# Splitting each weight slab with one cast and one subtraction of 128x2048 instead of two of each of 128x1024

## The chip, the cores and the metric

The kernel runs on one core of one Trainium2 chip. The metric is the device time of one execution in microseconds. Shown is the median of three timed runs; a profile of one further execution tells where its time goes.

## The reference

A causal decoder trunk of two layers over 256 tokens of width 2048, in float32. Cut to its core:

```python
for layer in range(DEPTH):                       # 2 layers
    h = _rmsnorm(x, mix_norm_g[layer])
    if layer % 2 == 0:                           # latent attention and causal pooling
        c_q, c_kv, k_rope, u_pool = jnp.split(h @ even_w_in[e], split_at, axis=-1)
        a = _mla(c_q, c_kv, k_rope, cos, sin, ...)      # widens the latents by w_uq, w_ukv, then attends
        b = _pool_mixer(u_pool, even_pool_w[e], even_pool_scale[e])
        x = x + jnp.concatenate([a, b], axis=-1) @ even_w_out[e]
    else:                                        # gated short convolution
        x = x + _short_conv(h, odd_w_in[o], odd_conv_w[o], odd_w_out[o])
    x = x + _mlp(_rmsnorm(x, mlp_norm_g[layer]), w_mlp_up[layer], w_mlp_down[layer])   # 2048 -> 8192 -> 2048
```

## The kernel before

**Tiling.** TensorE multiplies in fp32r, so each float32 matrix is written as a sum of two parts: `hi`, the value cast to fp32r, and `lo`, the rest. A product then takes hi times hi, hi times lo and lo times hi. Weights come from HBM as slabs of 1 MB: one DMA on SyncE's queue fills a `raw` tile of 128 partitions by 2048 floats, which is four row tiles of 128x512 (or eight of 128x256). `slab` (L123) issues the DMA and calls `halved` (L132), which splits the slab: for each part of `sub` row tiles, ScalarE casts it into a `hi` tile (L141) and VectorE subtracts into a `lo` tile (L142). Before, a part is half a slab, 128x1024, so a slab takes two casts and two subtractions. Only the eight slabs of the latent projection at the start are split otherwise (two parts of 128x1088, the first one in three pieces).

**Buffers.** `new_stage` (L77) opens the pools: `raws` has three buffers of 8 KB a partition, and `halves` has, for each of `hi` and `lo`, six buffers of 4 KB. A `hi` tile may be written again when TensorE has read its last use; a `raw` tile may be filled again when the last subtraction from it is done.

**Stages.** First the latent projection (L153), up to about 65 us. Then the pooling projection (L464): four groups of channels g = 3, 2, 1, 0, each of two slabs of eight row tiles; they are called G1 to G8 here. After each group VectorE takes the result from PSUM into `pu` (L479), GpSimd sums it over shifted copies into `pm` (L486 to L493), and ScalarE and VectorE split that (L201, L202). Then `widen` (L515) multiplies the latents by four slabs of w_ukv and three of w_uq, called W1 to W4 and Q1 to Q3: ScalarE takes each result out of PSUM (L522) and sums squares of it (L508), VectorE and GpSimd make the scale `rk` of it (L536, L277, L278), and VectorE applies it (L543, L546). Then come the pooling mixer with one slab, the attention mixed with the output projection, the MLP of layer 0 (about 300 to 940 us), the convolution, and the MLP of layer 1 (about 1355 to 1990 us).

**The MLP.** Sixteen chunks of 512 hidden columns go two and two. `up_chunk` (L719) multiplies four slabs of w_up; after each chunk its result is taken out of PSUM (`sum_halves`, L192), put through ReLU and the square (L732, L734) and split into `hT` (L201, L202), and sums of it into `fT`. `down_seven` (L751) makes a 2x2 block product of w_down in seven products instead of eight (`product`, L768, lines L772 to L774), from slabs and from blocks `t` and `v` to which GpSimd's queue adds further blocks of w_down while loading. The generators are called in an order written out by hand, which puts a slab of `up_chunk` (16 pairs of L161 and L162) behind each product (12 matmuls).

**Order.** Each engine runs its instructions in one order, fixed when the program is built, from the order in the code, the readiness of operands and buffers, and an estimate of durations. An instruction that waits holds up all that stand behind it on its engine.

Of the kernel before, what the change touches and what calls it, by code (L numbers as in the profile page):

```python
# [16 lines left out]
P = 128  # L17
# [15 lines left out]
GROUPS = 4  # L33
# [34 lines left out]
def trunk(ctx: ExitStack, tc, x_in, pos_in, mix_g, mlp_g, w_up, w_down, w_in, qa_g, kva_g, w_uq, w_ukv,  # L68
# [5 lines left out]
    big = ctx.enter_context(tc.tile_pool(name="big", bufs=1))  # L74
    stage = []

    def new_stage(raw_bufs=0, **more):  # L77

        for s_ in reversed(stage[1 - bool(raw_bufs):]):
            s_.close()  # L80
        del stage[1 - bool(raw_bufs):]
        for wanted in (dict(raws=raw_bufs, halves=6) if raw_bufs else {}, more):
            if wanted:
                stage.append(ExitStack())
                for name, bufs in wanted.items():
                    pools[name] = stage[-1].enter_context(tc.tile_pool(name=uid(name), bufs=bufs, reuse_waits="tile"))
# [8 lines left out]
    def uid(s):  # L95
        count[0] += 1
        return f"{s}{count[0]}"

    def bank2():
        return psum.tile([P, 2, 512], F32, tag="ps", name=uid("ps"))  # L100
# [6 lines left out]
    def flush():  # L107

        todo = waiting[:]
        waiting.clear()  # L110
        for f in todo:
            f()
# [7 lines left out]

    last_prep = []

    def slab(src, kt, cols, sub=2, dmas=1, pieces=None):  # L123

        raw = pools["raws"].tile([P, kt, cols], F32, tag="raw", name=uid("raw"))
        rows_ = src.rearrange("(k p) n -> p k n", p=P)
        for i in range(dmas):
            n = kt // dmas
            nc.sync.dma_start(raw[:, i * n:(i + 1) * n, :], rows_[:, i * n:(i + 1) * n, :])
        return halved(raw, sub, pieces)  # L130

    def halved(raw, sub=2, pieces=None):  # L132

        kt, cols = raw.shape[1], raw.shape[2]
        out_ = []
        for i in range(0, kt, sub):
            hi = pools["halves"].tile([P, sub, cols], F32R, tag="hi", name=uid("hi"))
            lo = pools["halves"].tile([P, sub, cols], F32R, tag="lo", name=uid("lo"))
            for c0, n in pieces if pieces and i == 0 else ((0, cols),):
                r, h, l = (w[:, :, c0:c0 + n] for w in (raw[:, i:i + sub, :], hi, lo))  # L140
                a = nc.scalar.copy(h, r)  # L141
                v = nc.vector.tensor_tensor(out=l, in0=r, in1=h.bitcast(F32), op=ALU.subtract)  # L142
            last_prep[:] = [a, v]
            out_ += [(hi[:, j, :], lo[:, j, :]) for j in range(sub)]
        return out_
# [12 lines left out]
    def columns_out(o, act, kt, w, c0, first, last):  # L158

        hi, lo = w  # L160
        nc.tensor.matmul(o, lhsT=hi[:, c0:c0 + P], rhs=act[:, kt, :], start=first, stop=False)  # L161
        nc.tensor.matmul(o[:, S:2 * S], lhsT=lo[:, c0:c0 + P], rhs=act[:, kt, 0:S], start=False, stop=last)  # L162

    def columns_summed(o, act, kt, w, c0, first, last):

        hi, lo = w
        nc.tensor.matmul(o, lhsT=hi[:, c0:c0 + P], rhs=act[:, kt, 0:S], start=first, stop=False)  # L167
        nc.tensor.matmul(o, lhsT=hi[:, c0:c0 + P], rhs=act[:, kt, S:2 * S], start=False, stop=False)  # L168
        nc.tensor.matmul(o, lhsT=lo[:, c0:c0 + P], rhs=act[:, kt, 0:S], start=False, stop=last)  # L169

    def columns_chunk(w, xT, c0, n):

        pss = []
        for _ in columns_steps(pss, w, xT, c0, n):
            pass
        return pss

    def columns_steps(pss, w, xT, c0, n):

        pss.extend(bank2() for _ in range(n // 2))  # L180
        rows_ = 16 // n
        for s in range(KD // rows_):
            ws = slab(w[s * rows_ * P:(s + 1) * rows_ * P, c0:c0 + n * P], rows_, n * P, sub=rows_ // 2)
            for j in range(rows_):
                kt = s * rows_ + j
                for i in range(n):
                    columns_out(pss[i // 2][:, i % 2, :], xT, kt, ws[j], i * P, kt == 0, kt == KD - 1)
            if s == 0:
                flush()
            yield  # L190
# [20 lines left out]
    attn = ExitStack()  # L211
    ap_ = attn.enter_context(tc.tile_pool(name="attn", bufs=1, side="right"))
    ctx.callback(lambda: [s_.close() for s_ in reversed(stage)])
    new_stage(3)


    x = big.tile([P, T, D], F32, tag="x", name="x")
# [105 lines left out]
    def twice(a):  # L323

        return a.unsqueeze(1).to_broadcast([P, 2, S])
# [9 lines left out]
    def latent_slab(s, insts=()):  # L335
        with behind(*insts):
            slabs.append(slab(w_in[0, s * 2 * P:(s + 1) * 2 * P, 0:LAT], 2, LAT, sub=1,
                              dmas=2 if s == 0 else 1, pieces=cuts if s == 0 else None))
# [3 lines left out]
    for s in range(8):  # L342
        if s:
            latent_slab(s)
        ws = slabs[s]
# [4 lines left out]
        for j in range(2):  # L350
            kt = 2 * s + j
# [40 lines left out]
    R0 = []  # L392
    waiting.append(latents)
    new_stage(3)

    PAD = 16
# [60 lines left out]
    def split_pooled(g, m):  # L457
        c, k = g // 2, 2 * (g % 2)
        if c not in pooledT:
            pooledT[c] = act_tile()  # L460
        split(pooledT[c][:, k:k + 2, 0:S], pooledT[c][:, k:k + 2, S:2 * S], m)

    done = None
    for g in reversed(range(GROUPS)):  # L464
        ps = bank2()
        for s in range(2):
            c0 = LAT + g * 2 * P
            ws = slab(w_in[0, s * 8 * P:(s + 1) * 8 * P, c0:c0 + 2 * P], 8, 2 * P, sub=4)
            for j in range(8):
                kt = 8 * s + j  # L470
                for n in range(2):
                    columns_summed(ps[:, n, 0:S], xT, kt, ws[j], n * P, kt == 0, kt == KD - 1)
            if s == 0:
                flush()
        if done:
            split_pooled(*done)
        u = ap_.tile([P, 2, PAD + S], F32, tag="s", name=uid("pu"), bufs=4)
        nc.gpsimd.memset(u[:, :, 0:PAD], 0.0)
        nc.vector.tensor_tensor(out=u[:, :, PAD:], in0=ps[:, :, 0:S], in1=twice(R0[0]), op=ALU.mult)  # L479
        cur = u  # L480
        for st in range(g + 1):
            sh = 1 << st
            nxt = ap_.tile([P, 2, PAD + S], F32, tag="s", name=uid("pn"), bufs=4)
            if st < g:
                nc.gpsimd.memset(nxt[:, :, 0:PAD], 0.0)
            nc.gpsimd.tensor_tensor(out=nxt[:, :, PAD:], in0=cur[:, :, PAD:], in1=cur[:, :, PAD - sh:PAD + S - sh],  # L486
                                    op=ALU.add)
            cur = nxt
        m = small.tile([P, 2, S], F32, tag="u", name=uid("pm"))
        nc.gpsimd.tensor_scalar(out=m, in0=cur[:, :, PAD:], scalar1=1.0 / (2 << g), scalar2=None, op0=ALU.mult)  # L490
        nc.gpsimd.tensor_tensor(out=m[:, :, 0:PAD], in0=cur[:, :, PAD:2 * PAD],
                                in1=invc[:, g, :].unsqueeze(1).to_broadcast([P, 2, PAD]), op=ALU.mult)
        nc.gpsimd.tensor_tensor(out=m, in0=m, in1=u[:, :, PAD:], op=ALU.subtract)  # L493
        done = g, m
# [34 lines left out]
    for b in range(4):  # L529
        widen(w_ukv, latT[0], 1, b, QW)  # L530
        tot = small.tile([P, T, 2], F32, tag="tot2", name=uid("tot"))
        for t in range(T):
            for h in (2 * b, 2 * b + 1):
                c0 = QW + h * (NOPE + VD)
# [39 lines left out]


    mixed = {}
    ws = slab(pool_w[0].rearrange("g c d -> (g c) d"), 2 * GROUPS, 2 * P, sub=4)
    for c in range(2):
        mt = act_tile()
        mixed[2 + c] = mt  # L580
        for i in range(2):
            g = 2 * c + i
# [129 lines left out]
    def mlp(layer, ss, xT, after=None):  # L712
        up, down = w_up[layer], w_down[layer]
        hid, sums, totals = {}, {}, {}
        r2 = []
        new_stage(blocks=1, forms=2)
        pairs = DFF // NB // 2

# [32 lines left out]
        def down_seven(pair):  # L751
# [16 lines left out]
            def product(o, b, left):  # L768

                for q, (hi, lo) in enumerate(halved(b)):  # L770
                    a_hi, a_lo = left(2 * pair + q // 2, q % 2)
                    nc.tensor.matmul(o, lhsT=a_hi, rhs=hi, start=q == 0, stop=False)  # L772
                    nc.tensor.matmul(o, lhsT=a_hi, rhs=lo, start=False, stop=False)  # L773
                    nc.tensor.matmul(o, lhsT=a_lo, rhs=hi, start=False, stop=q == 3)  # L774
# [207 lines left out]
```

## Time and profile before

| | |
|---|---|
| timed runs | 2027.75, 2026.78, 2024.16 us; median 2026.78 us |
| profiled execution | 2025.33 us, of which the span from the first to the last instruction is 2023.5 us |
| TensorE (PE) | 2005.9 us busy, 10534 matmuls |
| VectorE (DVE) | 1389.5 us busy, 1739 instructions |
| ScalarE (ACT) | 1120.1 us busy, 1480 instructions |
| GpSimd (POOL) | 124.4 us busy |
| DMA | 457.62 MB, 226 GB/s over the span |
| granted TensorE clock | 0.998 on the mean |

The matmuls overlap, so their busy time is a union and not a sum. The chain of work that ended last consists to 98% of matmuls. What counts is therefore the time at which TensorE stands still, and which engine it then waits for; the idle time of the other engines costs nothing by itself.

### The profile page before, as it was taken

Reading aid. Unit: us, or ns where it says so; the run is one execution under the profiler, and the core shown is the slowest. Engines: PE = TensorE matmul, PEld = TensorE weight load, DVE = VectorE, ACT = ScalarE, POOL = GpSimd, SP = SyncE. Lnnn points to the kernel's source line nnn. Section 1 sums busy time; section 2 is a strip of 40 time slices with the busy share of each in tenths; the row PEclk is TensorE's granted clock in tenths of the full one; section 3 lists DMA queues with packets and bytes.
Section 4 is the critical chain, followed back from the end, with each engine's and each line's share of the span. In section 5 each row is a group of like instructions: output and inputs, shape, how many; then the busy total and the mean of one; then the engine's idle time right before and its main releaser. Section 6 shows DMA issues by size and latency. Waiting matters only on the chain.

```text
span 2023.5 us, 26714 instructions
## 1 busy us (share of the span) xinstructions
PE 2005.9 (99%) x10534; PEld 1722.5 (85%) x10534; DVE 1389.5 (69%) x1739; ACT 1120.1 (55%) x1480; POOL 124.4 (6%) x132
## 2 busy tenths in 40 slices
PE   8999999999999999999999999999999999999999
PEld 7987888888888888888888888888888888888887
DVE  5767567677766777776666656567777777777774
ACT  5457456565555655555444444456555566555552
POOL 2240000000000000000000000000000000000000
PEclk9999999999999999999999999999999999999999
DMA  7555577998989889865555557758898988989773
GB/s 245 161 173 177 182 219 215 270 247 242 281 252 264 245 258 257 263 208 187 179 190 188 190 191 226 231 177 222 267 255 265 270 239 265 257 253 270 217 224 125
DMA packets 232782, 457.62 MB, mean 226 GB/s; under 512 B 7344, under 2 KB 17456, under 8 KB 232656
## 3 DMA queue, kind: packets, MB, share of 16 engines
q1 hardware_dynamic: 202704, 396.91, 58.5%
q0 software_dynamic: 29920, 59.00, 17.1%
q8 instruction: 82, 1.34, 0.3%
q14 instruction: 44, 0.36, 0.0%
q10 hardware_dynamic: 32, 0.01, 0.0%
HBM read 453.79 MB, written 2.10 MB: 225 GB/s over the span
## 4 chain that ended last, share of the span: by engine, by line
PE 98%; DMA 1%; ACT 1%; SPq 0%; issue 0%; DVE 0%; ACTq 0%
PE ps L161 32%; PE ps L162 16%; PE ps L154 11%; PE ps L155 11%; PE ps L156 11%; PE ps L772 4%; PE ps L774 4%; PE ps L773 4%; PE ps L167 1%; PE ps L168 1%; PE ps L169 1%; PE ps L298 1%; DMA raw<-in_even_w_in 1%; PE ps L615 0%; ACT hi L141 0%; PE ps L619 0%
## 5 line engine op out<-in xcount | busy, mean ns | idle before, releaser
L142 DVE TENSOR_TENSOR lo<-raw,hi 128x1024 fp32r<-128x1024 f32 (+2 forms) x694 | 847.8, 1227 | 413.9 <-ACT hi L141 409.6
L141 ACT CAST hi<-raw 128x1024 fp32r<-128x1024 f32 (+2 forms) x694 | 724.8, 1049 | 620.9 <-PE ps L161 285.2
L161 PE MATMUL ps<-xT,hi 128*128 128x512 f32 x2816 | 988.9, 394 | 0.0
L162 PE MATMUL ps<-xT,lo 128*128 128x256 f32 x2816 | 789.5, 280 | 0.0
L161 PEld LDWEIGHTS ps<-xT,hi 128*128 128x128 f32 x2816 | 529.5, 188 | 122.1
L162 PEld LDWEIGHTS ps<-xT,lo 128*128 128x128 f32 x2816 | 527.6, 187 | 3.7
L154 PE MATMUL ps<-hi,hT 128*128 128x512 f32 (+1 forms) x896 | 349.1, 390 | 0.0
L156 PE MATMUL ps<-hi,hT 128*128 128x512 f32 (+1 forms) x896 | 347.3, 388 | 0.0
L155 PE MATMUL ps<-lo,hT 128*128 128x512 f32 (+1 forms) x896 | 347.2, 388 | 0.0
L154 PEld LDWEIGHTS ps<-hi,hT 128*128 128x128 f32 x896 | 168.3, 188 | 35.1 <-issue 1.3
L156 PEld LDWEIGHTS ps<-hi,hT 128*128 128x128 f32 x896 | 168.2, 188 | 34.7
L155 PEld LDWEIGHTS ps<-lo,hT 128*128 128x128 f32 x896 | 168.3, 188 | 33.6 <-DVE lo L142 0.4
L142 DVE TENSOR_TENSOR lo<-t,hi 128x1024 fp32r<-128x1024 f32 x84 | 102.6, 1221 | 45.2 <-ACT hi L141 45.1
L141 ACT CAST hi<-t 128x1024 fp32r<-128x1024 f32 x84 | 87.3, 1051 | 73.2 <-PE ps L161 50.7
L766 POOL DMA_DIRECT2D t<-in_w_mlp_down x42 | 54.4, 1296 | 1107.0 <-DVE lo L142 720.3
L772 PE MATMUL ps<-hi,fT 128*128 128x512 f32 x224 | 88.1, 393 | 0.0
L774 PE MATMUL ps<-hi,fT 128*128 128x512 f32 x224 | 87.7, 391 | 0.0
L773 PE MATMUL ps<-lo,fT 128*128 128x512 f32 x224 | 87.1, 389 | 0.0
L195 ACT COPY t<-ps 128x512 f32<-128x512 f32 x88 | 50.9, 579 | 40.6 <-PE ps L162 40.4
L772 PE MATMUL ps<-hi,hT 128*128 128x512 f32 x168 | 65.8, 392 | 0.0
L774 PE MATMUL ps<-hi,hT 128*128 128x512 f32 x168 | 65.6, 391 | 0.0
L773 PE MATMUL ps<-lo,hT 128*128 128x512 f32 x168 | 65.4, 389 | 0.0
(186 smaller groups left out, 1582.3 us busy)
## 6 DMA issues: line engine op xcount, KB each, us to landing
raw<-in_w_mlp_up SPq DMA_DIRECT2D x128, 1024.0 KB, 7.2
raw<-in_w_mlp_down SPq DMA_DIRECT2D x114, 1024.0 KB, 6.4
raw<-in_odd_w_in SPq DMA_DIRECT2D x48, 1024.0 KB, 5.1
t<-in_w_mlp_down POOLq DMA_DIRECT2D x42, 1024.0 KB, 13.5
raw<-in_even_w_out SPq DMA_DIRECT2D x16, 1024.0 KB, 5.4
raw<-in_odd_w_out SPq DMA_DIRECT2D x16, 1024.0 KB, 5.3
t<-in_w_mlp_down SPq DMA_DIRECT2D x14, 1024.0 KB, 5.8
v<-in_w_mlp_down SPq DMA_DIRECT2D x14, 1024.0 KB, 5.8
```

The lines of the kernel that those rows point to most:

```text
L141: a = nc.scalar.copy(h, r)
L142: v = nc.vector.tensor_tensor(out=l, in0=r, in1=h.bitcast(F32), op=ALU.subtract)
L154: nc.tensor.matmul(o, lhsT=a_hi, rhs=hi[:, c0:c0 + n], start=first, stop=False)
L155: nc.tensor.matmul(o, lhsT=a_hi, rhs=lo[:, c0:c0 + n], start=False, stop=False)
L156: nc.tensor.matmul(o, lhsT=a_lo, rhs=hi[:, c0:c0 + n], start=False, stop=last)
L161: nc.tensor.matmul(o, lhsT=hi[:, c0:c0 + P], rhs=act[:, kt, :], start=first, stop=False)
L162: nc.tensor.matmul(o[:, S:2 * S], lhsT=lo[:, c0:c0 + P], rhs=act[:, kt, 0:S], start=False, stop=last)
L195: nc.scalar.copy(t, ps[:, :, S:2 * S])
L766: nc.gpsimd.dma_start(b, at(e, n), accum_op=ALU.add)
L772: nc.tensor.matmul(o, lhsT=a_hi, rhs=hi, start=q == 0, stop=False)
L773: nc.tensor.matmul(o, lhsT=a_hi, rhs=lo, start=False, stop=False)
L774: nc.tensor.matmul(o, lhsT=a_lo, rhs=hi, start=False, stop=q == 3)
```

## The change

A slab of four row tiles is cast and subtracted whole, and `halves` holds three buffers of 8 KB for each of `hi` and `lo` instead of six of 4 KB, so the same memory. The first stage, with the latent slabs, keeps its six smaller buffers and its parts. 788 casts and 788 subtractions of 128x1024 become 394 each of 128x2048. Matmuls and DMAs stay as many as they were.

```diff
-    def new_stage(raw_bufs=0, **more):
+    def new_stage(raw_bufs=0, half_bufs=3, **more):
...
-        for wanted in (dict(raws=raw_bufs, halves=6) if raw_bufs else {}, more):
+        for wanted in (dict(raws=raw_bufs, halves=half_bufs) if raw_bufs else {}, more):
...
-    def slab(src, kt, cols, sub=2, dmas=1, pieces=None):
+    def slab(src, kt, cols, sub=None, dmas=1, pieces=None):
...
-    def halved(raw, sub=2, pieces=None):
+    def halved(raw, sub=None, pieces=None):
 
         kt, cols = raw.shape[1], raw.shape[2]
+        sub = sub or kt
         out_ = []
         for i in range(0, kt, sub):
             hi = pools["halves"].tile([P, sub, cols], F32R, tag="hi", name=uid("hi"))
...
-            ws = slab(w[s * rows_ * P:(s + 1) * rows_ * P, c0:c0 + n * P], rows_, n * P, sub=rows_ // 2)
+            ws = slab(w[s * rows_ * P:(s + 1) * rows_ * P, c0:c0 + n * P], rows_, n * P)
...
-    new_stage(3)
+    new_stage(3, 6)
...
-            ws = slab(w_in[0, s * 8 * P:(s + 1) * 8 * P, c0:c0 + 2 * P], 8, 2 * P, sub=4)
+            ws = slab(w_in[0, s * 8 * P:(s + 1) * 8 * P, c0:c0 + 2 * P], 8, 2 * P)
...
-    ws = slab(pool_w[0].rearrange("g c d -> (g c) d"), 2 * GROUPS, 2 * P, sub=4)
+    ws = slab(pool_w[0].rearrange("g c d -> (g c) d"), 2 * GROUPS, 2 * P)
```

The change also moves instructions on ScalarE and VectorE; from here on, its line numbers are one higher than before. The first place is VectorE's order in the pooling projection, before: raw139 is slab G7, raw144 G8, raw157 W1, raw170 W2; `pm` is what GpSimd made of a group, and `pu` what it starts from.

```order
L142 TENSOR_TENSOR lo143_1143<-raw139_1136,hi142_1142 128x1024
L142 TENSOR_TENSOR lo146_1197<-raw144_1194,hi145_1196 128x1024
L202 TENSOR_TENSOR hT117_986<-pm122_1000,hT117_986 128x2x256
L142 TENSOR_TENSOR lo148_1201<-raw144_1194,hi147_1200 128x1024
L142 TENSOR_TENSOR lo159_1283<-raw157_1280,hi158_1282 128x1024
L479 TENSOR_TENSOR pu134_1123<-ps123_1004,R94_791 128x2x256
L142 TENSOR_TENSOR lo161_1287<-raw157_1280,hi160_1286 128x1024
L142 TENSOR_TENSOR lo172_1340<-raw170_1337,hi171_1339 128x1024
L202 TENSOR_TENSOR hT149_1252<-pm137_1131,hT149_1252 128x2x256
L142 TENSOR_TENSOR lo174_1344<-raw170_1337,hi173_1343 128x1024
```

The same place in the changed kernel, where raw127 is G7, raw130 G8, raw141 W1 and raw152 W2:

```order
L143 TENSOR_TENSOR lo129_1115<-raw127_1112,hi128_1114 128x2048
L203 TENSOR_TENSOR hT109_970<-pm114_984,hT109_970 128x2x256
L143 TENSOR_TENSOR lo132_1169<-raw130_1166,hi131_1168 128x2048
L480 TENSOR_TENSOR pu122_1099<-ps115_988,R92_787 128x2x256
L143 TENSOR_TENSOR lo143_1251<-raw141_1248,hi142_1250 128x2048
L203 TENSOR_TENSOR hT133_1220<-pm125_1107,hT133_1220 128x2x256
L143 TENSOR_TENSOR lo154_1304<-raw152_1301,hi153_1303 128x2048
L480 TENSOR_TENSOR pu134_1223<-ps126_1111,R92_787 128x2x256
```

Before, the first halves of G8 and of W2 stood ahead of the splits that wait for GpSimd; now both slabs stand behind them whole. On ScalarE their casts stand in the same way to the casts of `pm`.

The second place is VectorE's order a little later, before: raw183 is W3 and raw196 W4; the rows from `tot` to `qkv` make and apply the scale of W1's result.

```order
L142 TENSOR_TENSOR lo187_1401<-raw183_1394,hi186_1400 128x1024
L142 TENSOR_TENSOR lo198_1454<-raw196_1451,hi197_1453 128x1024
L536 TENSOR_SCALAR tot163_1317<-ksum_1265 128x2 x2
L277 TENSOR_SCALAR rv169_1329<-tot163_1317 128x4
L543 SCALAR_TENSOR_TENSOR qkv_1264<-qkv_1264,rk168_1328,both_675 128x128 x4
L546 TENSOR_TENSOR qkv_1264<-lat_587,rk168_1328 128x2x128
L142 TENSOR_TENSOR lo200_1458<-raw196_1451,hi199_1457 128x1024
```

In the changed kernel, where raw163 is W3 and raw174 W4:

```order
L143 TENSOR_TENSOR lo165_1357<-raw163_1354,hi164_1356 128x2048
L537 TENSOR_SCALAR tot145_1281<-ksum_1233 128x2 x2
L278 TENSOR_SCALAR rv151_1293<-tot145_1281 128x4
L544 SCALAR_TENSOR_TENSOR qkv_1232<-qkv_1232,rk150_1292,both_675 128x128 x4
L547 TENSOR_TENSOR qkv_1232<-lat_587,rk150_1292 128x2x128
L143 TENSOR_TENSOR lo176_1410<-raw174_1407,hi175_1409 128x2048
```

The scale of W1 stood between the two halves of W4; now all of W4 stands behind it, and so on for the slabs after it.

The third place is ScalarE's order in each MLP behind its second chunk, before the first product that needs that chunk's `hT`. Before, t504 is a block of w_down, raw524 a slab of w_up and raw530 one of w_down:

```order
L141 CAST hi521_3210<-t504_3133 128x1024
L732 ACTIVATE h496_3103<-h496_3103 128x512
L195 COPY t499_3116<-ps472_2930 128x512
L734 ACTIVATE sq497_3106<-h496_3103 128x512
L141 CAST hi525_3231<-raw524_3229 128x1024
L201 CAST hT493_3099<-sq497_3106 128x2x256
L732 ACTIVATE h500_3118<-h500_3118 128x512
L141 CAST hi527_3235<-raw524_3229 128x1024
L734 ACTIVATE sq501_3121<-h500_3118 128x512
L201 CAST fT494_3100<-f498_3110 128x512
L201 CAST hT493_3099<-sq501_3121 128x2x256
L141 CAST hi531_3274<-raw530_3272 128x1024
```

In the changed kernel, where t424 is the block and raw438 the slab of w_up:

```order
L142 CAST hi435_3038<-t424_2973 128x2048
L733 ACTIVATE h416_2943<-h416_2943 128x512
L196 COPY t419_2956<-ps400_2786 128x512
L735 ACTIVATE sq417_2946<-h416_2943 128x512
L202 CAST hT413_2939<-sq417_2946 128x2x256
L733 ACTIVATE h420_2958<-h420_2958 128x512
L202 CAST fT414_2940<-f418_2950 128x512
L735 ACTIVATE sq421_2961<-h420_2958 128x512
L202 CAST hT413_2939<-sq421_2961 128x2x256
L142 CAST hi439_3059<-raw438_3057 128x2048
```

The whole cast of the slab of w_up moved behind both casts of `hT`, between which its halves stood.

## Rows read from the trace of the kernel before

**Rows 1.** The page, part 1: busy time, share of the span, instructions of each engine.

```profile
PE 2005.9 (99%) x10534; PEld 1722.5 (85%) x10534; DVE 1389.5 (69%) x1739; ACT 1120.1 (55%) x1480; POOL 124.4 (6%) x132
```

**Rows 2.** Waits of TensorE: who waited for whom, us in total, times, longest.

```profile
PE ps L167 <- ACT qkv L522: 3.0, 1, 3.0
PE ps L167 <- ACT hi L141: 1.9, 1, 1.9
```

**Rows 3.** Stretches: length, busy us of each engine, granted clock, DMA share, GB/s.

```profile
160.00:165.00 5.00, 5.00 (x34) 4.89 (x33) 2.69 (x9) 3.91 (x18) 0.48 (x1) 0.74 0.38 148
300.00:940.00 640.00, 640.00 (x3263) 544.69 (x3262) 464.62 (x540) 376.53 (x445) 33.51 (x28) 1.00 0.85 247
```

**Rows 4.** Groups by line and shape: busy us, mean ns of one, idle before, releasers.

```profile
L142 DVE TENSOR_TENSOR lo<-raw,hi 128x1024 fp32r<-128x1024 f32 x676 | 827.1, 1229 | 399.9 <-ACT hi L141 395.6 <-PE ps L162 2.7
L141 ACT CAST hi<-raw 128x1024 fp32r<-128x1024 f32 x676 | 707.3, 1050 | 609.5 <-PE ps L161 285.2 <-PE ps L156 102.1 <-DMA raw<-in_w_mlp_down 60.6
...
L202 DVE TENSOR_TENSOR hT<-sq,hT 128x512 fp32r<-128x512 f32 x64 | 44.0, 688 | 30.2 <-ACT hT L201 30.2
...
L201 ACT CAST hT<-sq 128x512 fp32r<-128x512 f32 x64 | 39.6, 619 | 1.0
```

**Rows 5.** Timeline around G1: start us, us, engine, line, [idle before <-releaser].

```profile
66.58 2.01 ACT L141 CAST hi<-raw 128x1024 fp32r<-128x1024 f32 x2
67.68 2.36 DVE L142 TENSOR_TENSOR lo<-raw,hi 128x1024 fp32r<-128x1024 f32 x2 [1.60 <-ACT hi L141]
67.70 0.39 PE L167 MATMUL ps<-xT,hi 128*128 128x256 f32 x1 [1.94 <-ACT hi L141]
...
69.49 0.62 ACT L387 ACTIVATE junk<-lat 128x512 f32<-128x512 f32 x1
...
70.72 0.46 ACT L205 ACTIVATE hT<-ps,gains 128x256 fp32r<-128x256 f32 x1
...
75.39 0.36 PE L167 MATMUL ps<-xT,hi 128*128 128x256 f32 x1
```

**Rows 6.** Timeline around G8 and W2.

```profile
107.70 0.62 ACT L201 CAST hT<-pm 128x512 fp32r<-128x512 f32 x1 [8.61 <-POOL pm L493]
108.23 3.89 ACT L141 CAST hi<-raw 128x1024 fp32r<-128x1024 f32 x4
...
109.27 0.28 PE L169 MATMUL ps<-xT,lo 128*128 128x256 f32 x1
...
111.58 0.68 DVE L479 TENSOR_TENSOR pu<-ps,R 128x512 f32<-128x512 f32 x1
...
120.12 3.90 ACT L141 CAST hi<-raw 128x1024 fp32r<-128x1024 f32 x4
...
120.74 0.39 PE L155 MATMUL ps<-lo,hT 128*128 128x512 f32 x1
```

**Rows 7.** Timeline where W4 begins on TensorE, and its second subtraction.

```profile
131.62 0.39 PE L155 MATMUL ps<-lo,hT 128*128 128x512 f32 x1
...
132.75 2.36 DVE L142 TENSOR_TENSOR lo<-raw,hi 128x1024 fp32r<-128x1024 f32 x2
```

**Rows 8.** Timeline in the pooling mixer.

```profile
157.41 1.26 ACT L522 ACTIVATE qkv<-ps,lat_r 128x512 f32<-128x512 f32 x2
...
158.72 0.39 PE L167 MATMUL ps<-hT,hi 128*128 128x256 f32 x1 [3.01 <-ACT qkv L522]
```

**Rows 9.** Timeline at the first product of layer 0 that needs chunk 1.

```profile
328.63 0.62 ACT L201 CAST hT<-sq 128x512 fp32r<-128x512 f32 x1
...
329.30 0.50 PE L772 MATMUL ps<-hi,hT 128*128 128x512 f32 x1
```

**Rows 10.** Timeline at a slab of w_up in the MLP of layer 0.

```profile
627.05 1.05 ACT L141 CAST hi<-raw 128x1024 fp32r<-128x1024 f32 x1 [4.72 <-DMA raw<-in_w_mlp_up]
...
632.03 0.40 PE L161 MATMUL ps<-xT,hi 128*128 128x512 f32 x1
```

**Rows 11.** Waits of SyncE's DMA queue: us in total, times, longest.

```profile
SPq L129 <- DVE lo L142: 1228.5, 248, 12.0
```

## The prediction

> **What bounds the kernel now.** I read the busy times first [rows 1]. TensorE is busy for 2005.9 of 2023.5 us; ScalarE with 55% and VectorE with 69% have room. So the span is TensorE's own work plus some 18 us in which it stands still, and a change that leaves its 10534 matmuls alone can only take from those 18 us or add to them. Next I read whom TensorE waits for [rows 2]. Waits that this change can touch are two: 1.9 us for the first cast of the pooling projection, and 3.0 us in the pooling mixer for ScalarE's L522. The other idle time lies in the first 20 us, where the latent slabs are not changed, and at the end, where the last results are stored. In the MLP TensorE has no idle time at all: 640.00 us busy of 640.00 [rows 3]. There is thus no stall there to remove, and the question is whether the change makes one.
>
> **What a cast and a subtraction cost.** From 512 to 1024 columns a cast goes from 619 to 1050 ns and a subtraction from 688 to 1229 ns [rows 4]. The same slope leads to 1050 + 2 x 431 = 1912 ns and 1229 + 2 x 541 = 2311 ns at 2048. From above the bound is twice the row, 2100 and 2458 ns. I take 1.9 and 2.3 us. A pair that runs back to back already takes only 2.01 and 2.36 us [rows 5], so 394 slabs save ScalarE some 40 us and VectorE some 20 us of busy time, on engines that have room. On the path to TensorE that is worth nothing.
>
> [...]
>
> What changes is when TensorE may begin. Before, half a slab is ready 1.05 + 1.23 = 2.3 us after its cast begins. Now the whole slab must be ready: 1.9 + 2.3 = 4.2 us. The buffers also come free later: a half waited for the half six before it, that is 2.5 slabs of TensorE's work ahead, a whole slab waits for the slab three before it, 2 slabs ahead. Where TensorE's slab takes 5.4 to 5.6 us (24 matmuls at 0.227 us, the two slabs W2 and W3 from 120.74 to 131.62 [rows 6, 7]), two slabs are 11 us and cover the 4.2. So the price falls only where ScalarE or VectorE comes late anyway. I go through these places; "late" is against the clock of the profiled execution.
>
> *G1.* TensorE waits from 65.8 to 67.70 for the first cast, which began at 66.58 [rows 5]. A cast of 1.9 us ends 0.85 us later: **+0.85**. Its subtraction is hidden by the 18 transposes that TensorE has there.
>
> *G2.* TensorE begins it at 75.39, now 76.2. In the new order the cast stands behind four sums of squares at 0.8 us (0.62 and a read of 0.19) and three splits at 0.46 [rows 5]: 68.5 + 4.6 = 73.1, cast to 75.0, subtraction to 77.4. The first lo is wanted at 76.45: **+0.95**. TensorE is 1.8 us late from here.
>
> *G8.* The cast of `pm` at 107.70 waited 8.61 us for GpSimd, and the casts of G8 behind it start at 108.23 [rows 6]. GpSimd is about 1 us later, since the subtraction ahead of its input is whole now. The cast of G8 then runs from 109.3 to 111.2 and the subtraction to 113.6. TensorE wants lo at 109.27 + 1.8, plus some 0.4 us that it was already held for hi: **+2.1**, late 3.9 in all.
>
> *W2.* The next `pu` (111.58 before [rows 6]) comes at 113.6, so the cast of `pm` ends 2 us later, and W2's cast starts at 122.2 instead of 120.12. It is done at 124.1, the subtraction at 126.5. TensorE wants lo at 120.74 + 3.9 = 124.6: **+1.85**, late 5.75.
>
> *W4 to Q3.* W4's second half was subtracted from 132.75 behind the scale of W1, and its first half long before; TensorE began at 131.62 [rows 7]. Now the whole slab starts where the second half stood. GpSimd's last group is 3.2 us late by its `pu`, so the subtraction ends at 132.75 + 3.2 + 2.3 = 138.3, against 131.62 + 5.75 = 137.4: **+0.95**. By the same steps Q1 is just in time, Q2 loses **+0.7**, Q3 nothing. Sum of the first layer: +7.4 us.
>
> *What comes back.* At 158.72 TensorE ended its wait of 3.01 us for L522 at 157.41, which stood behind the sums of squares of Q2 and two casts of the output projection [rows 8]. TensorE now arrives some 7.4 us later, and in my walk ScalarE's copy of Q3 comes only 4 us later, before TensorE needs the bank: the wait goes, **-3.0**. [...] Without the wait I expect no such stretch there: **-1.3**. The net of the first layer is +3.1 us. [...]
>
> *The first product of each MLP that needs its second chunk.* The cast of hT ended 0.05 us before TensorE wanted it at 329.30 [rows 9]. In the new order the subtraction of the whole block t stands ahead of hT's subtraction, and the cast of the next w_up slab stands behind both casts of hT, where its halves stood between them. I get waits of 0.15, 0.35 and 0.3 us for the parts of hT, and 0.95 us for the cast of the slab, of which TensorE's order wants two matmuls right behind. **+1.75**, in each of two layers: +3.5 us.
>
> *The rest of the MLP.* The tightest slab of w_up landed at 627.05 and TensorE wanted it at 632.03 [rows 10]: 5.0 us for what now takes 4.2, while SyncE's next DMA waits for the subtraction that frees its buffer [rows 11], 1.9 us later than before. If the landing moves by all of that, TensorE waits 1.1 us. Other pairs have such a slab too, with about 1 us more room, so most are just covered. I take **+1.5** for 14 pairs, between 0 and 14 x 1.1 = 15.
>
> **Sum.** 3.1 + 3.5 + 1.5 = +8.1 us on the profiled execution's 2025.3: 2033.4. That execution is 1.45 us below the median of the runs shown; on that median the sum is 2034.9. I say 2034.
>
> **Rivals.** *Hidden after all.* The walk through the first layer adds errors of a microsecond at each step. If the slabs W4 and Q2 are covered, the first four waits give 5.75 and the return 4.3; if hT's slab is also in time, the total is +1.5: 2028. For it speaks that two slabs of work lie between a buffer and its use; against it that G1's 0.85 is certain and that the orders put whole slabs behind waits. *The MLP's cover breaks.* If DMAs that are issued 1.9 us later land later by that and contention, two slabs in each of the 14 pairs may miss by about 1 us: +28 less what the other terms share, 2050 to 2060. For it speaks that ScalarE already waited 4.72 us for a landing [rows 10] and that DMA is busy at 0.85 [rows 3]; against it that TensorE has never waited there. It decides from the point where the landing moves by more than 0.8 us at most pairs. *Faster.* The larger operations let ScalarE and VectorE run ahead: only G1's 0.85 stays, while the 3.0 and the 1.3 us and the short wait of some 0.4 us behind them vanish: -3.9, 2023; with no price at the products. It decides if whole slabs are ready before TensorE at G8 and W2, that is if GpSimd's groups end 2 us sooner than in my walk. [...] *The operations do not get cheaper.* At 2.1 and 2.46 us a slab is 0.3 us later at each of some ten places: +3, within the forecast's range.
>
> **How the numbers follow.** The forecast, 2029 to 2041, gets 0.47; hidden, 2025 to 2029, gets 0.25; the MLP's break, 2041 to 2060, gets 0.18; faster gets 0.10. About 0.2%, 4 us, is what a measurement of this kernel can tell from no change, so faster means below 2022.7 and slower above 2030.8. A fifth of the forecast's chance lies between 2029 and 2030.8. Faster takes 0.08 of its 0.10. Slower takes 0.38 of the forecast and the 0.18, with a little of hidden: 0.58. The same takes the rest, 0.34. The range of 8 in 10 takes the forecast, most of hidden and the lower third of the break: 2025 to 2044.
>
> **What would show it.** A cast of 1.9 and a subtraction of 2.3 us in the groups. TensorE's waits after: about 2.8 us for the first cast at G1 instead of 1.9; waits for L142 (lo) at G2, G8, W2 and W4 that were not there; no 3.0 us wait for L522; the clock near 1.0 over 155 to 170; waits of TensorE for hT or hi near 330 and 1380. In the MLP elsewhere TensorE's busy time should fill its stretches. Wrong I would be if TensorE's idle time moved by other amounts at other places, above all by waits in every pair of the MLP, or if the matmuls themselves took another time.

## The result and the profile after

The changed kernel takes 2037.6 us (median of 4 runs, 2036.46 to 2039.68) against 2025.86 us (4 runs, 2024.16 to 2027.75): 1.0058 times the time before, 95% interval 1.0045 to 1.007. It is slower by 11.7 us; the forecast of 2034 and +8.1 us had the sign, and its range holds the time. The profiled execution took 2036.46 us, 11.13 us more than the one of before. Its busy times, and then the groups of the split by line and shape (busy us, mean ns of one, idle before, releasers), which answer to [rows 1] and [rows 4]:

```profile
PE 2011.8 (99%) x10534; PEld 1722.2 (85%) x10534; DVE 1345.7 (66%) x1345; ACT 1060.0 (52%) x1086; POOL 124.8 (6%) x132
```

```profile
L143 DVE TENSOR_TENSOR lo<-raw,hi 128x2048 fp32r<-128x2048 f32 x338 | 773.2, 2290 | 422.1 <-ACT hi L142 421.6
L142 ACT CAST hi<-raw 128x2048 fp32r<-128x2048 f32 x338 | 645.6, 1911 | 533.1 <-PE ps L162 194.1 <-DMA raw<-in_w_mlp_down 86.4 <-PE ps L157 70.5
```

A cast takes 1.91 us and a subtraction 2.29 us, as forecast from the slope. VectorE has 44 us less to do and ScalarE 60 us less, and the kernel is slower. The waits of TensorE show where a part of that is; [rows 2] had two of these lines (us in total, times, longest):

```profile
PE ps L168 <- ACT hi L142: 3.6, 2, 2.8
...
PE ps L170 <- DVE lo L143: 1.8, 1, 1.8
PE ps L162 <- ACT hi L142: 1.0, 2, 0.5
PE ps L155 <- DVE rT L611: 0.9, 1, 0.9
PE ps L156 <- DVE lo L143: 0.7, 2, 0.5
...
PE ps L773 <- ACT p L790: 0.5, 2, 0.3
PE ps L773 <- ACT hT L202: 0.5, 2, 0.2
PE ps L163 <- DVE lo L143: 0.3, 1, 0.3
```

These waits are short, and TensorE's busy time went up by 5.9 us besides. To place the rest I paired the matmuls of the two traces in the order of their starts, the nth with the nth: both hold 10534 of them, and the start of one here less its start before, each counted from the start of its span, tells how far the changed kernel is behind. The list gives that lag at places of [rows 5 to 10], in us:

| place in the trace of before | lag | what was added since the line above |
|---|---|---|
| 65, latent projection done | 1.62 | the start, which moves from one execution to the next (1.12 in a second execution of the kernel before, -0.74 in one of the changed kernel) |
| 67.70, G1 | 2.47 | +0.85 |
| 109.27, ahead of G8's waits | 1.24 | -1.23, without a wait: the pooling's matmuls ran closer (+0.08 in the second execution) |
| 120, ahead of W2's lo | 5.70 | +4.46: at G8 0.93 for hi and 1.98 for lo, the rest the lower clock behind them |
| 131.62, W4 | 6.86 | +1.16: W2 0.35, W4 0.64, and small ones |
| 158.72, pooling mixer | 3.85 | -3.17 (and +0.16 ahead of it) |
| 163.98 | 1.85 | -2.00: a short wait of 0.5 is gone, and so is the lower clock of [rows 3] (-1.36) |
| 165.03 | 2.92 | +1.07, of it 0.97 a wait for rT |
| 345, behind the first product with chunk 1 | 4.96 | +2.03 |
| 990, convolution begins | 5.78 | +0.82 over the rest of the MLP, 0.46 at the slab of [rows 10] |
| 1250, convolution ends | 8.96 | **+3.18, with no wait of TensorE in it** |
| 1400, product of layer 1 | 11.02 | +2.06 |
| end | 11.15 | +0.13 |

So the change costs 1.3 us in the first layer (2.92 - 1.62), 4.1 at the two products, 1.0 in the rest of the MLPs, and 3.2 in the convolution stage, which the prediction didn't name. Another execution of the same kernel (below) began 2.4 us earlier and gives nearly the same sums: 1.35, 4.1 and 3.2, with 2.3 in the rest of the MLPs. Its first layer comes to its sum in another way: no gain in the pooling and no lower clock behind G8, but 1.7 at G8 and 1.7 at W2.

The timeline around G1 and G8, for [rows 5] and [rows 6] (start, us, engine, line; in brackets the idle time before and what ended it):

```profile
68.21 1.91 ACT L142 CAST hi<-raw 128x2048 fp32r<-128x2048 f32 x1
...
70.15 2.29 DVE L143 TENSOR_TENSOR lo<-raw,hi 128x2048 fp32r<-128x2048 f32 x1 [2.45 <-ACT hi L142]
...
70.17 0.39 PE L168 MATMUL ps<-xT,hi 128*128 128x256 f32 x1 [2.78 <-ACT hi L142]
...
109.61 3.70 ACT L142 CAST hi<-raw 128x2048 fp32r<-128x2048 f32 x2
...
111.54 2.29 DVE L143 TENSOR_TENSOR lo<-raw,hi 128x2048 fp32r<-128x2048 f32 x1 [1.11 <-ACT hi L142]
...
111.56 0.39 PE L168 MATMUL ps<-xT,hi 128*128 128x256 f32 x1 [0.77 <-ACT hi L142]
...
113.89 0.58 PE L170 MATMUL ps<-xT,lo 128*128 128x256 f32 x1 [1.82 <-DVE lo L143]
```

TensorE waits for the whole cast, does its two hi products, and then waits for the whole subtraction. Behind that the granted clock fell, to 0.50 from 114 to 116, as it had before in 160 to 165 [rows 3], with 0.50 from 160 to 162; there it is now 1.00 (stretches: length, busy us of each engine, clock, DMA share, GB/s):

```profile
110.00:115.00 5.00, 2.41 (x15) 2.00 (x14) 3.88 (x4) 3.31 (x2) 0.48 (x1) 0.85 0.01 4
115.00:120.00 5.00, 5.00 (x37) 5.00 (x37) 1.64 (x1) 0.00 (x0) 4.90 (x4) 0.81 0.99 325
...
160.00:165.00 5.00, 5.00 (x41) 4.92 (x40) 3.89 (x5) 5.00 (x23) 0.00 (x0) 1.00 0.59 190
```

And the first product of layer 0 that needs chunk 1 [rows 9], ScalarE and then TensorE:

```profile
335.60 0.62 ACT L202 CAST hT<-sq 128x512 fp32r<-128x512 f32 x1
336.13 1.90 ACT L142 CAST hi<-raw 128x2048 fp32r<-128x2048 f32 x1
```

```profile
336.28 0.50 PE L773 MATMUL ps<-hi,hT 128*128 128x512 f32 x1 [0.21 <-ACT hT L202]
...
338.08 0.72 PE L162 MATMUL ps<-xT,hi 128*128 128x512 f32 x2 [0.50 <-ACT hi L142]
339.08 0.50 PE L773 MATMUL ps<-hi,fT 128*128 128x512 f32 x1 [0.28 <-ACT p L790]
```

The whole cast of w_up's slab begins behind the cast of hT and ends at 338.03; the matmul that wants it starts at 338.08.

### The profile page after: what moved, and what is told of

It reads as the page before. It is cut to its first block, busy times and chain, and to the rows that moved or that the text cites. A ratio compares the mean times of both kernels' runs of the same rounds, so it can differ in the third digit from the quotient of the medians.

```text
span 2034.7 us, 25439 instructions
## 1 busy us (share of the span) xinstructions
PE 2011.8 (99%) x10534; PEld 1722.2 (85%) x10534; DVE 1345.7 (66%) x1345; ACT 1060.0 (52%) x1086; POOL 124.8 (6%) x132
## 4 chain that ended last, share of the span: by engine, by line
PE 93%; ACT 2%; POOL 2%; DMA 1%; DVE 1%; issue 1%; SPq 0%; ACTq 0%; POOLq 0%
PE ps L162 32%; PE ps L163 16%; PE ps L155 10%; PE ps L156 10%; PE ps L157 10%; PE ps L773 4%; PE ps L775 4%; PE ps L774 4%; ACT hi L142 1%; POOL pn L487 1%; DMA raw<-in_even_w_in 1%; PE ps L299 1%; DMA raw<-in_w_mlp_up 1%; DVE lo L143 1%; POOL pm L491 0%
## 5 line engine op out<-in xcount | busy, mean ns | idle before, releaser
L143 DVE TENSOR_TENSOR lo<-raw,hi 128x2048 fp32r<-128x2048 f32 (+2 forms) x356 | 793.8, 2233 | 437.6 <-ACT hi L142 437.2
L162 PE MATMUL ps<-xT,hi 128*128 128x512 f32 x2816 | 992.4, 395 | 1.0 <-ACT hi L142 1.0
L142 ACT CAST hi<-raw 128x2048 fp32r<-128x2048 f32 (+2 forms) x356 | 663.1, 1865 | 546.1 <-PE ps L162 194.1
L162 PEld LDWEIGHTS ps<-xT,hi 128*128 128x128 f32 x2816 | 529.2, 188 | 125.0 <-ACT hi L142 1.6
L143 DVE TENSOR_TENSOR lo<-t,hi 128x2048 fp32r<-128x2048 f32 x42 | 96.1, 2289 | 52.5 <-ACT hi L142 52.5
L142 ACT CAST hi<-t 128x2048 fp32r<-128x2048 f32 x42 | 80.2, 1911 | 63.8 <-PE ps L162 49.8
L198 DVE TENSOR_TENSOR h<-ps,t 128x512 f32<-128x512 f32 x64 | 44.0, 687 | 35.6 <-ACT t L196 35.6
```

## The experiments

The theory: each wait comes from the size of an operation that stands behind something late, whereas the 3.2 us of the convolution stage are a pace of TensorE's that has nothing to do with the split's operations beside it. Rivals: the coarser buffers cost the time, or TensorE is slowed by the larger operations beside it, or the differences are chance. Beside the three groups of runs below the kernel before took 2027.27, 2027.45 and 2027.2 us (medians of 15, 26 and 27 runs), so the ratios are what compares.

**The two kernels once more**, unchanged, one profiled execution each.

> The changed kernel once more, for how far one execution stands for all. Theory (late slabs plus a pace of TensorE that is set at the start of the convolution stage): TensorE's waits at G1, G8, W2 and W4 and at the first product of each MLP come back within 0.3 us each, and the pairs of matmuls of the convolution stage take 353.3 ns again, since order and waits are the same. Rival (the pace is chance from one execution to the next): the pairs take 348.9 ns here. The 1.6 us by which the first 65 us were longer should not come back, since nothing is changed there: 2034 to 2038 us.

> The kernel before once more. Theory: pairs of matmuls at 353 ns from the start of the convolution stage to the two transposes there, then 348.9 ns, as in the first profile; waits of 1.9 and 3.0 us in the first layer. Rival (chance): the pace in the convolution stage differs from the first profile. 2024 to 2028 us either way, 3 us more if the pace is the slow one.

2035.57 and 2026.29 us. The waits return at the same places (G1 2.8 us, G8 1.5, W2 and W4 2.0 together), without the lower clock behind G8. At G8 and W2 they differ from the first execution (2.6 and 0.2 us there, 1.5 and 1.5 here) by more than the 0.3 us expected. The convolution stage takes the same 3.2 us more. The counts of matmuls in its middle 220 us tell it (the same columns as above; a pair is L161 and L162, one line higher in the changed kernel); first the kernel before again, then the changed kernel as first profiled:

```profile
1020.00:1240.00 220.00, 220.00 (x1263) 192.67 (x1263) 139.80 (x172) 95.82 (x103) 0.62 (x6) 1.00 0.57 187
```

```profile
1020.00:1240.00 220.00, 220.00 (x1247) 191.81 (x1246) 135.94 (x133) 88.06 (x65) 0.61 (x6) 1.00 0.57 184
```

TensorE is busy all the time at a granted clock of 1.00 in both, and does 16 matmuls more in one than in the other. From start to start a pair takes 348.9 ns before and 353.3 after (mean of the pairs). Ahead of the two transposes of the norm's factor, at 995.60 and 1000.39 below, both kernels run at the longer one; the kernel before leaves it there, the changed one does not. What differs there is tiny. The kernel before, again, and then the changed kernel, behind the transposes:

```profile
995.60 0.38 PE L318 MATMUL ps<-ident,rb 128*128 128x128 f32 x2
...
996.51 0.45 PE L161 MATMUL ps<-xT,hi 128*128 128x512 f32 x1
996.79 0.28 PE L162 MATMUL ps<-xT,lo 128*128 128x256 f32 x1
```

```profile
1000.39 0.38 PE L319 MATMUL ps<-ident,rb 128*128 128x128 f32 x2
...
1001.29 0.50 PE L162 MATMUL ps<-xT,hi 128*128 128x512 f32 x1
1001.63 0.28 PE L163 MATMUL ps<-xT,lo 128*128 128x256 f32 x1
```

The third hi matmul takes 0.45 us in one and 0.50 in the other, and from there the pace differs for 250 us.

**One transpose more** at the start of that stage of the changed kernel; its result is not used.

```diff
     def over_tokens(r, pool, extra=0):
...
+        for k in range(extra):
+            nc.tensor.transpose(ps[:, 1, k * P:(k + 1) * P], rb, ident)
...
-            R1.append(over_tokens(r1sq, conv_pool))
+            R1.append(over_tokens(r1sq, conv_pool, 1))
```

> The changed kernel with one more 128x128 transpose, of no use, behind the two at the start of the convolution stage. Theory (pace set by how TensorE comes out of that spot): the pairs take 348.9 instead of 353.3 ns for some 250 us, 3.1 us less, 2034.4 us; if the transpose does not happen to move it over, nothing changes. Rival (the slow pace comes from the whole-slab casts and subtractions running beside it): 353.3 ns for the whole stage, 2037.6 us.

2035.6 us, ratio 1.0045 (1.0032 to 1.0058). The stage is at 348.9 ns a pair from the transposes on, 1263 matmuls in the same stretch, with the same whole casts and subtractions beside it. So the rival that the larger operations slow the matmuls falls. By the ratios the time is 0.13% less than the changed kernel's, 2.6 us where 3.1 were expected, and the two intervals overlap; in time the effect shows better below.

**Two operations again, in the new buffers.** Each slab keeps its one pair of 8 KB tiles, but is cast and subtracted in two parts of 128x1024.

```diff
+    parts = [2]
...
-            for c0, n in pieces if pieces and i == 0 else ((0, cols),):
-                r, h, l = (w[:, :, c0:c0 + n] for w in (raw[:, i:i + sub, :], hi, lo))
+            m = parts[0] if sub == kt else 1
+            for k0 in range(0, sub, sub // m):
+                for c0, n in pieces if pieces and i == 0 else ((0, cols),):
+                    r, h, l = (w[:, k0:k0 + sub // m, c0:c0 + n] for w in (raw[:, i:i + sub, :], hi, lo))
```

> The changed kernel with its three whole buffers, but each slab filled by two casts and two subtractions of 128x1024. Theory (the slab is late because nothing can be used until 2048 columns are cast and subtracted, and because whole slabs stand behind other work): the waits for hi and lo at G8, W2, W4 and the products fall to under 0.5 us each, G1's wait is 1.9 us again; the 3.0 us wait for L522 comes back; 2026 to 2031 us depending on the pace of the convolution stage. Rival (the later release of the buffers is what costs): waits as in the changed kernel, 2035 to 2039 us.

2027.24 us, ratio 0.9999 (0.999 to 1.0008). G1 is back at 1.9 us, and of the waits for the split only 0.3 us at W4 are left:

```profile
PE ps L171 <- ACT hi L145: 1.9, 1, 1.9
...
PE ps L159 <- DVE lo L146: 0.3, 1, 0.3
```

So the size of the operations made the waits, not the buffers. (More buffers than three weren't tried.) But one expectation was wrong: the 3.0 us wait for L522 [rows 8] did not come back, though TensorE is not late here. By the lag this kernel gains 3.95 us in the first layer, and loses 3.2 in the convolution stage (1245 matmuls in the stretch); with the start left out it ends 0.9 us ahead of the kernel before, which the interval of the ratio leaves open. That account is of the execution profiled, the shortest of the 11 (2023.68 us at a mean granted clock of 0.999; the median, 2027.24, had 0.997). Against this trace, at the same pace in the convolution stage, whole slabs cost 5.3 us in the first layer, 4.1 at the two products and 1.0 to 2.3 in the rest of the MLPs. ScalarE around the copies of Q2 and Q3:

```profile
148.58 1.27 ACT L526 ACTIVATE qkv<-ps,lat_r 128x512 f32<-128x512 f32 x2 [2.69 <-PE ps L160]
...
151.86 1.99 ACT L145 CAST hi<-raw 128x1024 fp32r<-128x1024 f32 x2
...
154.06 1.24 ACT L526 ACTIVATE qkv<-ps,lat_r 128x512 f32<-128x512 f32 x2
```

Here the two casts of the first output-projection slab stand behind the copy and the sums of squares of Q2. In the kernel before, the first of them stands ahead of the copy; its second execution shows what that does:

```profile
151.72 1.05 ACT L141 CAST hi<-raw 128x1024 fp32r<-128x1024 f32 x1 [2.35 <-DMA raw<-in_even_w_out]
152.68 1.26 ACT L522 ACTIVATE qkv<-ps,lat_r 128x512 f32<-128x512 f32 x2
...
158.29 1.25 ACT L522 ACTIVATE qkv<-ps,lat_r 128x512 f32<-128x512 f32 x2
```

ScalarE stands 2.35 us at a cast (here for the slab's DMA, in the first execution 2.46 us for its buffer), the copy of Q2 is 3 us late, and the copy of Q3 after it. In the changed kernel, too, no cast of that slab stands ahead of the copy of Q2, which now waits for TensorE:

```profile
155.18 1.27 ACT L523 ACTIVATE qkv<-ps,lat_r 128x512 f32<-128x512 f32 x2 [2.65 <-PE ps L157]
...
158.47 1.89 ACT L142 CAST hi<-raw 128x2048 fp32r<-128x2048 f32 x1
...
160.80 1.24 ACT L523 ACTIVATE qkv<-ps,lat_r 128x512 f32<-128x512 f32 x2
```

**That one cast moved** in the kernel before: it is told to be issued behind Q2's sums of squares. TensorE's order stays as it was. As built, two later casts and one subtraction come later too, so it is not quite one thing that moved.

```diff
-                ws = slab(w[row * 4 * P:(row + 1) * 4 * P, b * NB:(b + 1) * NB], 4, NB)
+                ws = slab(w[row * 4 * P:(row + 1) * 4 * P, b * NB:(b + 1) * NB], 4, NB,
+                          after=first if b == 0 and i == 0 else ())
...
-        return halved(raw, sub, pieces)
+        with behind(*after):
+            return halved(raw, sub, pieces)
```

> The kernel before, with one thing moved: on ScalarE the cast of the first half of the first output-projection slab stands behind the copy of Q2 and its sums of squares, not ahead of them. If the 3.0 us wait for L522 came from that cast, which waited 2.46 us for a half's buffer while the copy of Q2 stood behind it, the wait goes, with the 0.5 us behind it and the stretch at the lower clock: 2021.5 to 2023.5. Rival, that the wait goes only where TensorE comes later (as the prediction had it): no change, 2026 to 2027.5.

2023.93 us, ratio 0.9984 (0.9975 to 0.9993), a little above the 2021.5 to 2023.5 expected. The wait for L522 is gone, and with it the lower clock of 160 to 165 (1.00 there now); behind it 0.9 us of waiting for hT (L207) stand where 0.4 did. The lag falls by 3.9 us between 150 and 165 and, behind the start, moves nowhere else. The rival, that the wait goes only where TensorE comes later, falls.

**Whole slabs in one half of the program.** Two parts up to the first MLP and whole slabs from there on; and whole slabs except in the two MLPs. Both use the loop of the two-part kernel; the edit shown is that of the first.

```diff
         new_stage(blocks=1, forms=2)
+        parts[0] = 1
```

> Two casts and two subtractions of 128x1024 per slab in layer 0 up to its MLP, whole slabs from the first MLP on. If each wait comes from the size of the operations where they are late, the waits at G8 and W2 vanish and G1's falls to 1.9 us, so the first layer is some 5 us shorter than in the changed kernel; the two products that need the second chunk still cost 2 us each, and the convolution stage is still at the slow pace of its matmuls: 2031 to 2033. Rival, the cost lies in the MLP alone: 2035 to 2037.

> The other half: two parts of 128x1024 only in the two MLPs, whole slabs before and between them. By size alone the waits at the two products and at the tight slab of w_up vanish (2 x 2.05 + 0.5 = 4.6 us), while G1, G8, W2 and W4 stay as in the changed kernel and the convolution stage stays slow: 2032 to 2033. Rival, that what comes late at the products comes late because the first layer was late: 2035 to 2037.

2033.37 us, ratio 1.0026 (1.0018 to 1.0035), and 2033.21 us, ratio 1.0027 (1.0018 to 1.0037). Both lie a little above their forecasts (2031 to 2033, 2032 to 2033) and below their rivals'. TensorE's waits in the two, those of the start left out:

```profile
PE ps L171 <- ACT hi L145: 1.9, 1, 1.9
PE ps L165 <- ACT hi L145: 1.0, 2, 0.5
...
PE ps L777 <- ACT p L794: 0.5, 2, 0.3
PE ps L777 <- ACT hT L205: 0.5, 2, 0.2
PE ps L159 <- DVE lo L146: 0.4, 1, 0.4
```

```profile
PE ps L171 <- ACT hi L145: 2.8, 1, 2.8
...
PE ps L159 <- DVE lo L146: 2.0, 2, 1.5
PE ps L173 <- DVE lo L146: 1.6, 1, 1.6
PE ps L158 <- DVE rT L614: 0.9, 1, 0.9
```

The first has the products' waits and not the first layer's, the second the reverse. In the second TensorE never waits in an MLP (busy 625.00 of 625.00 us over 345 to 970, 600.00 of 600.00 over 1400 to 2000), though the first layer is late: the two costs don't depend on each other. In time, too, the savings against the changed kernel, 0.32 and 0.31%, add up to about the 0.59% of two parts everywhere. Both are still at the longer pace in the convolution stage (1581 and 1580 matmuls over 970 to 1250, where the two-part kernel with one transpose more, below, has 1596).

**Only the cast whole, or only the subtraction.**

```diff
                 a = nc.scalar.copy(h, r)
+                m = 2 if sub == kt else 1
+                for k0 in range(0, sub, sub // m):
+                    rk, hk, lk = (w[:, k0:k0 + sub // m] for w in (r, h, l))
-                v = nc.vector.tensor_tensor(out=l, in0=r, in1=h.bitcast(F32), op=ALU.subtract)
+                    v = nc.vector.tensor_tensor(out=lk, in0=rk, in1=hk.bitcast(F32), op=ALU.subtract)
```

> One cast of 128x2048 per slab, but two subtractions of 128x1024. Where TensorE waits for lo, the first half is ready some 1.1 us sooner: W2 and W4 lose their short waits and G8 some 1 us, and the products' waits for lo shrink; waits for hi (2.8 us at G1) stay. If the subtraction is the half that costs: 2031 to 2033. Rival, the whole cast is what costs (TensorE's waits are mostly for hi): 2034 to 2037.

> Two casts of 128x1024 per slab and one subtraction of 128x2048. Where TensorE waits for hi, the first half is ready 0.85 us sooner: G1 falls back to 1.9 us, the wait for the slab behind the products to about 0.1 us; waits for lo at G8, W2 and W4 stay, the convolution stage stays slow: 2034 to 2035. If what costs is how late the raw buffers come free, as more waits of slabs for their DMAs suggested in the kernel with one cast and two subtractions: the same as the changed kernel, 2035.5 to 2037.5.

2039.61 us, ratio 1.0054 (1.004 to 1.0067), and 2037.21 us, ratio 1.0051 (1.0039 to 1.0064). Neither takes back anything that can be told from the whole change: the first forecasts (2031 to 2033, and 2034 to 2035) were wrong. The rival of the first run, 2034 to 2037, misses its time as well, and its reason, that the whole cast is what costs, falls with the second run, where casts in halves gain nothing. The rival of the second, 2035.5 to 2037.5, holds its time. Where the first half came sooner a wait did shrink (G1 falls to 1.9 us with two casts; with two subtractions G8 has no wait for lo), but others came. TensorE's waits for slabs of w_up in the two:

```profile
PE ps L166 <- DVE lo L146: 2.0, 4, 0.8
...
PE ps L165 <- ACT hi L142: 1.0, 2, 0.5
```

```profile
PE ps L165 <- DVE lo L145: 3.5, 7, 0.9
```

In the changed kernel the waits for lo there were 0.3 us in 1 (1.3 in 3 in its second execution). Both profiled executions are at the slow end of their five runs (2041.85 of 2036.49 to 2041.85 us, and 2040.21 of 2034.36 to 2040.24), so a usual one may have fewer such waits.

Why others came stays open. With one cast and two subtractions ScalarE's casts wait 186 us in all for slabs of the MLPs to land, against 132 in the changed kernel, which would fit `raw` buffers that come free later. But with two casts and one subtraction they wait only 63 us, and that kernel is no faster. SyncE's queue doesn't tell either: over all that it waits for, it stands 1879 and 1872 us in the two, 1875 in the changed kernel and 1856 in the two-part kernel. A later release of `raw` wasn't tried alone.

**Two parts, and the pace.** The two-part kernel with one and with two transposes more, and the kernel before with one.

> Two parts everywhere in the new buffers, and one transpose more (its result unused) at the start of the convolution stage. If a short disturbance moves TensorE's pairs of matmuls there from the slow pace (353.3 ns a pair) to the fast one (348.9), the stage is 3.2 us shorter than in the two-part kernel: 2023 to 2024.5, slightly below the kernel before. If the pace depends on something else, 2027.

> Two parts everywhere and two transposes more at the start of the convolution stage instead of one. If any disturbance there leaves the slow pace, the stage is fast again: 2023 to 2024.5. If it depends on how the matmuls fall behind the transposes, it may stay slow: 2026.5 to 2027.5.

> The kernel before with one transpose more at the start of the convolution stage. It already runs that stage at the fast pace. If any disturbance moves the pace either way, it may fall to the slow one: 2029 to 2030.5. If only the slow pace is left by a disturbance, or if the transpose simply costs its own time: 2026 to 2027.5.

2023.37 us, ratio 0.9978 (0.9969 to 0.9987); 2027.06 us, ratio 0.9998 (0.9989 to 1.0007); 2027.32 us, ratio 0.9998 (0.9989 to 1.0007). The stretch 1020 to 1240 with one transpose more, then with two:

```profile
1020.00:1240.00 220.00, 220.00 (x1262) 192.62 (x1261) 136.22 (x169) 92.51 (x104) 0.62 (x6) 1.00 0.58 189
```

```profile
1020.00:1240.00 220.00, 220.00 (x1247) 191.51 (x1246) 135.64 (x170) 91.04 (x102) 0.62 (x6) 1.00 0.58 187
```

One transpose more brings the shorter pace, two don't, and the intervals of the times lie apart. In the kernel before, with one more, the stage keeps the shorter pace (1263). So a disturbance does not just end the longer pace; it can leave either pace behind it. The two-part kernel with one transpose more is faster than both kernels of the change.

## Why the prediction was right, point by point

- **The operations** cost 1.91 and 2.29 us, as taken. They save ScalarE 60 and VectorE 44 us of busy time (forecast some 40 and 20). On the path that is worth nothing: two parts in the same buffers are as fast as before (ratio 0.9999), whole slabs 0.58% slower.
- **First layer, new waits** (forecast 7.4). G1 was right to the hundredth, 0.85. G2 and Q2 cost nothing (forecast 0.95 and 0.7). G8 took 2.9 (2.1), W2 0.35 (1.85; 1.7 in the second execution), W4 0.64 (0.95). The rT wait of 0.97 behind the mixer wasn't forecast; it is there in the five profiles whose first layer has whole casts, and in no other. The lower clock behind G8 cost about 1.5 us in one execution and nothing in the other. With 1.2 us that the pooling matmuls gained in that same execution, the net is +1.3, as it is without either in the other, where I had +3.1: each step of the walk was off by up to 1.5 us, and most were too high.
- **What comes back** was right in size, -3.17 and -1.36 (forecast -3.0 and -1.3), and wrong in its reason; that is luck, since the wait goes whole whatever removes it. The 1.3 is (1 - 0.74) x 5 us over the stretch 160 to 165 of [rows 3]; in that trace the clock is 0.50 from 160 to 162, 0.68 to 163 and 1.00 behind it, in the changed kernel 1.00 throughout. Counted from the end of the latent projection, TensorE came 5.4 us later there and the copy of Q3 1.8 (forecast 7.4 and 4). I took the wait to go because TensorE comes later. But in the two-part kernel TensorE is only 1.2 us later, and with the one cast moved it is on time, and the wait goes too: it is enough that the cast ahead of Q2's copy moves behind it, so that ScalarE comes earlier against TensorE. Whether TensorE's lateness alone would have done it wasn't tried.
- **The products** cost 2.03 and 2.06 (forecast 1.75 each), by the waits that the order showed: hT, the slab's cast, and `p` behind that.
- **The rest of the MLPs** took 1.0 (2.3 in the second execution; forecast 1.5), and 0.46 of it at the tightest slab. The rival of the MLP's broken cover fell.
- **The step that failed** is the sentence that leaving the matmuls alone leaves only TensorE's idle time to change. In the convolution stage the same matmuls took 3.2 us longer with no wait. TensorE's busy time rose by 5.9 us. The last line of the prediction named another time of the matmuls as what would make it wrong, without a price. The forecast of +8.1 and the measured +11.1 of the profiles differ by this 3.2 and by 1.6 of the start, less the 1.8 of the first layer; products and MLPs nearly cancel. So that 2034 came near is in part luck: the first layer, taken too high, stands against the convolution stage, left out.
- **The rivals.** That all is hidden, or that it gets faster, fell with the waits at G1, G8 and the products. That the operations don't get cheaper fell with their times. The two-part kernel shows what was right in the faster one: with ScalarE's order of the new buffers and no new waits the first layer does gain 3.95 us, where that rival had 3.9.

## What to carry to other kernels

Here, where neither ScalarE nor VectorE is the bound, the first half of a slab being ready sooner was worth more than fewer operations (2027.24 against 2037.6 us), but only with both the cast and the subtraction in halves. The price of whole slabs fell at the few places where an engine was late already: the order of instructions finds them, the trace tells how late. When an order changes, look as well for what no longer stands ahead of a copy that TensorE needs. And pair the matmuls of two traces by their start times: that shows time which no wait explains.

## What the hardware did that I had not expected

Here a pair of fp32r matmuls of 512 and 256 columns, at a granted clock of 1.00 and with no wait, takes 348.9 or 353.3 ns on the mean from start to start, and keeps one pace for up to 250 us. Each pace is a cycle of three pairs: about 349, 347 and 351 ns, or 348, 357 and 355. In all 14 profiles the pairs of the MLPs (median 349 ns) and the first 16 pairs of the convolution stage (349.1 ns on the mean in the traces of before and after) run at the shorter one, and the 48 pairs behind the eight transposes that follow those 16 run at the longer (355.1 ns there). Behind the next two transposes, those of the norm's factor, it is one or the other. Without an added transpose it was the shorter in the three profiles with the buffers of before, and the longer in the seven with the new ones. With no, one and two transposes more the two-part kernel ran the stage at the longer, the shorter and the longer pace; the changed kernel at the longer with none and the shorter with one; the kernel before at the shorter with none and with one. What sets it stays open.
